# Branch projections by seven products of halves, with the weight sums of gates and branches kept in HBM

## The chip, the cores and the metric

The kernel runs on one core of a Trainium2 chip. The metric is the device time of one execution in microseconds (us). Three runs of the kernel before took 737.32, 737.47 and 738.17 us; the median is 737.47 us.

## The reference, cut to what matters

The program is one layer of a token mixer and a feed-forward block on an input of 512 tokens by 1024 channels, all in float32. Three mixers give `ya`, `yb` and `yc`, each 512 by 512. Each goes through a branch projection and is weighed by a gate:

```python
h = _rmsnorm(x, norm_mix[l])
p = h @ w_in[l]
u, v, bg, cg, xb, zc, gl = jnp.split(p, splits, axis=-1)
...
g = jax.nn.sigmoid(gl).reshape(bn, s, N_BRANCH, D_MODEL)
merged = (g[:, :, 0] * (ya @ w_br_a[l])
          + g[:, :, 1] * (yb @ w_br_b[l])
          + g[:, :, 2] * (yc @ w_br_c[l]))
x = x + merged @ w_o[l]
h = _rmsnorm(x, norm_ffn[l])
a = _causal_dwconv(h @ w_up[l], ffn_conv_w[l])
ag, av = jnp.split(a, 2, axis=-1)
x = x + (jax.nn.silu(ag) * av) @ w_down[l]
```

`w_br_*` are 512 by 1024, each gate's part of `w_in` is 1024 by 1024, `w_o` is 1024 by 1024, `w_up` is 1024 by 5632 and `w_down` 2816 by 1024.

## The kernel before, in words

**Arithmetic.** Every float32 operand of a matmul is split into a high part (a rounded copy by ScalarE, `upper`, line 59) and a low part (the rest, by VectorE, `lower`, line 67). One product of a 128x128 block with 128x512 columns is then three matmuls, high by high, high by low and low by high (`mm3`, lines 81 to 83).

**Stages**, in the order of the work: the head (x is turned, v is projected), ten column blocks of the input projections (u, z, cg, xb, bg; 1 MB of `w_in` each as two loads of 512 KB), three rounds of a gate and a branch projection, the output projection (`po`), eleven pairs of blocks of the up projection (`pug`, `puv`), the down projection (`da`, `dd`, `db`, `de`, `df`) and the final norm.

**Gates.** A gate's 512x1024 by 1024x1024 product is made of seven products of halves instead of eight (lines 877 to 925): tokens in two halves, k in two halves, output columns in two halves. The sums of activations are made on VectorE (`form`, lines 712 to 777). The sums of weights are made while loading: GpSimd issues DMAs that add a quarter of `w_in` to a buffer already in SBUF (`add_weights`, line 749; `gate_pieces`, lines 824 to 854). Each of the seven products is four k blocks of 128 by 512 columns, times two token blocks.

**Branches.** A branch projection is done plainly (lines 950 to 966): for each of two halves of 512 columns, four k blocks times four token blocks, `mm3` each. The projection comes after its gate; `weigh` (line 940) multiplies its PSUM bank with the gate on VectorE and adds it to the sum.

**Weights on their way.** `Raws` (lines 95 to 121) issues loads on SyncE's queue (line 109) in a fixed order, into buffers `raw` of 128x1024; a load is issued when the buffer it takes has been split. Four buffers are live in the input and up stages and eight in the gate stage (`raws.cap`, lines 781 and 967). `Pieces` (lines 247 to 267) splits a piece up to three ahead of its use into a ring; in the gate stage the ring is four slots of 128x512, in the up and down stages four slots of 128x1024.

**GpSimd.** Beside the adding DMAs it has some elementwise work in the input stage: `v - mu` (line 437), `row1_sq` (line 577), the four sums of the longest pooling window (line 633) and `cv * row1` (line 700). Its DMAs and what has to keep its place among them are chained by `in_order` (line 741).

**Down projection.** It uses seven products of halves too. Its four weight sums `t1` to `t4` are made in HBM by DMAs that GpSimd issues: a copy of a quarter of `w_down`, then a DMA that adds another quarter or sum to it (lines 1019 to 1022). They are 2816 KB each and run after the last gate's adding DMAs. SyncE later loads `t1` to `t4` as it loads weights.

Of the kernel before, what the change touches and what calls it, by code (L numbers as in the profile page):

```python
# [7 lines left out]
F32 = mybir.dt.float32  # L8
# [18 lines left out]
def trunk_kernel(  # L27
# [58 lines left out]
    RAWS = 8  # L86
# [3 lines left out]
    def extra_slots(name):  # L90

        return [[rawp.tile([P, 1024], F32R, tag="raw", name=f"{name}_{p}{i}") for p in ("hi", "lo")]
                for i in range(2)]
# [29 lines left out]
    raws = Raws()  # L123

# [51 lines left out]
    w_br = [w[0].rearrange("(k p) c -> p k c", p=P) for w in (w_br_a, w_br_b, w_br_c)]  # L176
# [9 lines left out]

    def rows(name, view, k, c0):
        raws.add(name, view[:, k:k + 2, c0:c0 + 512])
# [15 lines left out]
    for i in range(3):  # L204
        g0 = 3072 + 1024 * i

        for name, kh, h in (("w", 0, 0), ("x", 0, 0), ("v", 1, 0), ("y", 0, 1), ("z", 1, 1)):
            for kp in range(2):
                rows(f"g{i}{name}{kp}", w_in_v, 4 * kh + 2 * kp, g0 + 512 * h)
        for h in range(2):  # L210
            for kp in range(2):
                rows(f"br{i}{h}{kp}", w_br[i], 2 * kp, 512 * h)
    for h in range(2):
        for kq in range(4):
            rows(f"o{h}{kq}", w_o_v, 2 * kq, 512 * h)
    for name, view, c0 in col_blocks[n_in:]:
        cols(name, view, c0)

# [28 lines left out]
    class Pieces:  # L247
        def __init__(self, slots, ahead):
            self.slots, self.n_ahead = slots, ahead
            self.sources, self.done, self.taken = [], 0, 0  # L250
# [25 lines left out]
    first = extra_slots("first")  # L276
    slots = own + first
# [35 lines left out]
    load_v(6, 2)  # L313

# [118 lines left out]
    def v_center():  # L433
        nc.vector.tensor_scalar(mu, mu, 1.0 / 64, None, op0=ALU.mult)
        for t in range(NT):
            v3 = by_group(vs[t])
            nc.gpsimd.tensor_tensor(v3, v3, spread_group(mu, t), op=ALU.subtract)
# [101 lines left out]
    v_center()  # L539

# [25 lines left out]
    for b in range(2):  # L566
        w = blocks.take(f"u{b}")
        for j in range(2):
# [28 lines left out]
    ya = [pair(f"ya{c}", f"ya{c}") for c in range(4)]  # L597

    def spatial(q):
# [15 lines left out]
        nc.vector.tensor_tensor(t0, t0, uT[q], op=ALU.mult)  # L615
        split(ya[q][0], ya[q][1], t0)


    yc = [pair(f"yc{c}", f"yc{c}") for c in range(4)]
    PAD = 16  # L620

    def pooled(g, o):
# [6 lines left out]
        for step in range(g + 1):  # L629
# [3 lines left out]
            (nc.gpsimd if g == 3 else nc.vector).tensor_tensor(s2[:, lo:], s[:, lo:], s[:, lo - d:PAD + S - d], op=ALU.add)  # L633
# [11 lines left out]
    def pool_map(g, plr):  # L645
        o2 = bank(f"pyc{g}")
        mm3(o2, [p[:, g * P:(g + 1) * P] for p in pw], plr, True, True)
        nc.scalar.activation(yc[g][0], o2, AF.Copy, scale=p_scale(g))
        nc.vector.scalar_tensor_tensor(
            yc[g][1], o2, p_scale(g), yc[g][0].bitcast(F32), op0=ALU.mult, op1=ALU.subtract  # L650
        )
# [13 lines left out]
    yb = [pair(f"yb{c}", f"yb{c}") for c in range(4)]  # L665
    for b in range(2):
# [29 lines left out]
        for j in range(2):  # L696
# [13 lines left out]


# [17 lines left out]

    temps = iter(("x01", "x10", "x11", "x20", "x21", "x30", "x31", "x01"))  # L730
# [4 lines left out]
    def tt(o, a, b, op):  # L735
        return nc.vector.tensor_tensor(o, a, b, op=op)


    last_of_pool = []

    def in_order(ins):
        if last_of_pool:
            tc.add_manual_dep(
                ins.ins, last_of_pool.pop().ins.name,
                mybir.DependencyInfo(mybir.DependencyClass.NoSync, mybir.DependencyReason.DATA),
                reason="in the order written")
        last_of_pool.append(ins)

    def add_weights(t, view):
        in_order(nc.gpsimd.dma_start(t.rearrange("p (a b) -> p a b", b=view.shape[2]), view, accum_op=ALU.add))  # L750
# [28 lines left out]
    halves = [[t[:, 512 * c:512 * c + 512] for t in s] for s in own for c in range(2)]  # L779
    pieces = Pieces(halves, 3)  # L780
    raws.cap = RAWS

    def plain_piece(name, k, last, after=None):

        held = {}

        def source(slot):
            raw = raws.get(name) if k == 0 else source.raw()
            held["raw"] = raw
            split(*slot, raw[:, 512 * k:512 * k + 512])  # L790
            if last:
                raws.free()
            if after:
                after()

        source.held = held
        return source

    def block_pieces(name, after=None):
        a = plain_piece(name, 0, False)  # L800
        b = plain_piece(name, 1, True, after)
        b.raw = lambda: a.held["raw"]
        pieces.add(a)
        pieces.add(b)

# [489 lines left out]
```

## Time and profile before

| | |
|---|---|
| median of 3 runs | 737.47 us |
| the profiled execution, its own time | 737.11 us |
| its span on the core | 735.2 us |
| TensorE matmul (PE) busy | 725.7 us, 99% |
| VectorE (DVE) busy | 538.6 us, 73% |
| ScalarE (ACT) busy | 344.6 us, 47% |
| GpSimd (POOL) busy | 65.6 us, 9% |
| DMA queue q1 (issued by SyncE and ScalarE) | 88.90 MB, 38.1% of 16 engines |
| DMA queue q0 (issued by GpSimd) | 35.65 MB, 23.0% of 16 engines |

The page calls the engines PE, DVE, ACT, POOL and SP. Matmuls overlap, so that one of 128x512 is shown as lasting 389 ns while the next starts some 0.23 us later; time on TensorE is counted here by starts. A view of a stretch ("window") gives times from the start of the span. In the rows, a name like `pug` stands for all tiles of that name, `<-` separates what is written from what is read, and `L109` is a line of the kernel.

### The profile page before, as it was taken

The numbers are of one execution on the slowest core, as the hardware profiler recorded it, in microseconds if no ns is written. First come the engines' busy times: TensorE is split into PE (matmuls) and PEld (weight loads), VectorE is DVE, ScalarE is ACT, GpSimd is POOL, SyncE is SP. The second block draws the span as 40 slices with busy tenths as digits, with TensorE's granted clock in tenths as the row PEclk, the third lists the DMA queues.
The fourth block names the chain that finished last, engine by engine and source line by source line (L and its number), as shares of the span: only waits on it lengthen the run. The fifth ranks groups of instructions, "written<-read, shape, count | busy, mean of one in ns | idle before, by whom it ended". The sixth has DMA issues, their size and how long they took to land.

```text
span 735.2 us, 9006 instructions
## 1 busy us (share of the span) xinstructions
PE 725.7 (99%) x3294; PEld 600.9 (82%) x3294; DVE 538.6 (73%) x841; ACT 344.6 (47%) x537; POOL 65.6 (9%) x74
## 2 busy tenths in 40 slices
PE   8999999999999999999999999999999999999996
PEld 6888888888888888888888888888888888888885
DVE  6789799656556676765666886766787776998684
ACT  4744243246435525624544443443444444966453
POOL 0030202320121112101010000000000000001010
PEclk9999999999999999999999999999999999999999
DMA  7643122889879779999999963323233222576652
GB/s 256 183 138 92 52 87 84 202 198 232 228 157 214 198 169 193 365 249 360 234 241 313 221 180 101 100 86 115 87 92 108 87 101 86 153 240 194 193 164 115
DMA packets 79627, 126.24 MB, mean 172 GB/s; under 512 B 3639, under 2 KB 38879, under 8 KB 79583
## 3 DMA queue, kind: packets, MB, share of 16 engines
q1 hardware_dynamic: 64527, 88.90, 38.1%
q0 software_dynamic: 14336, 35.65, 23.0%
q10 hardware_dynamic: 720, 1.11, 0.4%
q8 instruction: 26, 0.43, 0.3%
q14 instruction: 18, 0.15, 0.1%
HBM read 120.41 MB, written 25.17 MB: 198 GB/s over the span
## 4 chain that ended last, share of the span: by engine, by line
PE 98%; DVE 1%; DMA 1%; ACT 0%; issue 0%; ACTq 0%
PE pug L83 5%; PE puv L83 5%; PE pug L81 5%; PE puv L81 5%; PE puv L82 5%; PE pug L82 5%; PE pbr L81 3%; PE pbr L82 3%; PE pbr L83 3%; PE po L81 2%; PE po L83 2%; PE po L82 2%; PE gb L82 1%; PE gb L81 1%; PE gd L82 1%; PE gd L81 1%
## 5 line engine op out<-in xcount | busy, mean ns | idle before, releaser
L81 PE MATMUL pug<-h2T_hi,second_hi 128*128 128x512 f32 x176 | 68.7, 390 | 0.0
L83 PE MATMUL pug<-h2T_hi,second_lo 128*128 128x512 f32 x176 | 68.5, 389 | 0.0
L82 PE MATMUL puv<-h2T_lo,ring_hi 128*128 128x512 f32 x176 | 68.5, 389 | 0.0
L81 PE MATMUL puv<-h2T_hi,ring_hi 128*128 128x512 f32 x176 | 68.5, 389 | 0.0
L82 PE MATMUL pug<-h2T_lo,second_hi 128*128 128x512 f32 x176 | 68.5, 389 | 0.0
L83 PE MATMUL puv<-h2T_hi,ring_lo 128*128 128x512 f32 x176 | 68.5, 389 | 0.0
L67 DVE TENSOR_TENSOR ring_lo<-raw_uv,ring_hi 128x1024 fp32r<-128x1024 f32 x22 | 26.9, 1221 | 25.1 <-ACT ring_hi L59 25.1
L59 ACT CAST second_hi<-raw_ug 128x1024 fp32r<-128x1024 f32 x22 | 23.2, 1055 | 43.1 <-PE pug L82 42.3
L82 PEld LDWEIGHTS puv<-h2T_lo,ring_hi 128*128 128x128 f32 x176 | 33.0, 188 | 6.9
L83 PEld LDWEIGHTS pug<-h2T_hi,second_lo 128*128 128x128 f32 x176 | 33.0, 188 | 6.9
L82 PEld LDWEIGHTS pug<-h2T_lo,second_hi 128*128 128x128 f32 x176 | 33.0, 188 | 6.9
L83 PEld LDWEIGHTS puv<-h2T_hi,ring_lo 128*128 128x128 f32 x176 | 33.0, 188 | 6.9
L81 PEld LDWEIGHTS puv<-h2T_hi,ring_hi 128*128 128x128 f32 x176 | 33.0, 188 | 6.9
L81 PEld LDWEIGHTS pug<-h2T_hi,second_hi 128*128 128x128 f32 x176 | 33.0, 188 | 6.8
L1142 POOL TENSOR_TENSOR xr<-xr,gain_f 128x512 f32<-128x512 f32 (+1 forms) x5 | 7.6, 1529 | 312.1 <-ACT sf L145 312.1
L67 DVE TENSOR_TENSOR ring_lo<-raw_br,ring_hi 128x512 fp32r<-128x512 f32 x24 | 16.6, 690 | 21.6 <-ACT ring_hi L59 21.6
L59 ACT CAST ring_hi<-raw_uv 128x1024 fp32r<-128x1024 f32 x22 | 23.2, 1054 | 19.2 <-PE puv L82 19.0
L67 DVE TENSOR_TENSOR second_lo<-raw_ug,second_hi 128x1024 fp32r<-128x1024 f32 x22 | 26.9, 1222 | 3.1 <-ACT second_hi L59 3.0
L1036 ACT ACTIVATE av<-av_y,colv 128x512 f32<-128x512 f32 x22 | 15.9, 724 | 27.9 <-DVE av_y L1034 26.9
L59 ACT CAST ring_hi<-raw_br 128x512 fp32r<-128x512 f32 x24 | 14.9, 620 | 26.0 <-PE pbr L83 18.8
L1036 ACT ACTIVATE ag<-ag_y,colv 128x512 f32<-128x512 f32 x22 | 15.7, 717 | 21.5 <-DVE ag_y L1034 21.5
L81 PE MATMUL po<-ring_hi,mg_hi 128*128 128x512 f32 x64 | 25.7, 401 | 0.0
(537 smaller groups left out, 2056.6 us busy)
## 6 DMA issues: line engine op xcount, KB each, us to landing
down_t<-in_w_down_dram POOLq DMA_DIRECT2D x6, 2816.0 KB, 27.9
raw_ug<-in_w_up_dram SPq DMA_DIRECT2D x22, 512.0 KB, 3.6
raw_uv<-in_w_up_dram SPq DMA_DIRECT2D x22, 512.0 KB, 3.5
raw_m<-down_t SPq DMA_DIRECT2D x20, 512.0 KB, 4.3
raw_m<-in_w_down_dram SPq DMA_DIRECT2D x15, 512.0 KB, 4.0
down_t<-down_t POOLq DMA_DIRECT2D x2, 2816.0 KB, 21.5
raw_o<-in_w_o_dram SPq DMA_DIRECT2D x8, 512.0 KB, 10.7
raw_u<-in_w_in_dram SPq DMA_DIRECT2D x4, 512.0 KB, 3.5
```

Of the source, the lines that this page charges most:

```text
L59: return keep(nc.scalar.copy(hi, src))
L67: return keep(nc.vector.tensor_tensor(lo, src, hi.bitcast(F32), op=ALU.subtract))
L81: keep(nc.tensor.matmul(o, st[0], mv[0], start=first, stop=False, **skip))
L82: keep(nc.tensor.matmul(o, st[0], mv[1], start=False, stop=False, **skip))
L83: keep(nc.tensor.matmul(o, st[1], mv[0], start=False, stop=last, **skip))
L1036: nc.scalar.activation(a, y, AF.Copy, scale=ffn_w(2, c))
L1142: nc.gpsimd.tensor_tensor(y, y, gain3[h][:, cut], op=ALU.mult)
```

## The change

It does these things:

- A branch projection is made of seven products of halves (`branch`), each of two k blocks times two token blocks, from sums of activations (`branch_forms`) and of weights. It now comes ahead of its gate, and its results `c` wait in SBUF; the gate multiplies them in. `ya`, `yb` and `yc` are no longer split, their forms are.
- In gate, branch and down projection the products M1, M6, M7 and M4 go into one PSUM bank pair `x` (M1 with its sign turned by its weights), which is copied out between (`copies`); M5 and M3 share another, M2 has a third.
- All weight sums of gates and branches are made in HBM (`WeightSums`): four tiles `t1` to `t4` for each, copied (`copy`) and added to (`add`) by DMAs of GpSimd. The copies for the first branch are issued once the last load of v's weights is there, the rest in a row after `v_center`. The adding DMAs into SBUF go away.
- Gate and branch weights are loaded and split as pieces of 128x1024, in a ring of four slots; the ring takes four more of the raw buffers for good, and four raw buffers are left.
- The down projection's sums are issued once x has been loaded again for the residual (`pool_waits_for`), copy and add by turns as before.
- The elementwise work of lines 577, 633 and 700 goes from GpSimd to VectorE.
- The output projection takes its k blocks in the order 4 to 7, 0 to 3, with some of the transposes (`turn`) within the gate and between its steps.

The diff, cut to its core:

```diff
-    RAWS = 8
+    own += [[rawp.tile([P, 1024], F32R, tag="raw", name=f"ring_{p}{i}") for p in ("hi", "lo")]
+            for i in range(2, 4)]
...
+    class WeightSums:
+        def __init__(self, name, b11, b12, b21, b22):
+            t1, t2, t3, t4 = self.t = [
+                dram.tile([P, b11.shape[1], 528], F32, name=f"{name}_t{i + 1}")[:, :, :512] for i in range(4)]
+            self.base = [(t1, b11), (t3, b12), (t2, b22), (t4, b21)]
+            self.added = [(t1, b12), (t3, b22), (t2, t1), (t4, t2)]
+
+            self.products = (("m1", b11), ("m5", t1), ("m6", t2), ("m2", b21), ("m7", t3), ("m3", b22), ("m4", t4))
+
+        def copy(self, n=4):
+            for t, w in self.base[:n]:
+                in_order(nc.gpsimd.dma_start(t, w))
+            del self.base[:n]
+
+        def add(self, n=4):
+            for t, w in self.added[:n]:
+                in_order(nc.gpsimd.dma_start(t, w, accum_op=ALU.add))
+            del self.added[:n]
...
     class Pieces:
...
         def take(self, n=1):
-
             i = self.taken
             self.taken += n
-            self.ahead(i + max(n, 1 + self.n_ahead))
-            got = [self.slots[k % len(self.slots)] for k in range(i, i + n)]
-            return got if n > 1 else got[0]
+            self.ahead(i + len(self.slots))
+            return [self.slots[k % len(self.slots)] for k in range(i, i + n)]
...
+    pool_waits_for(wv_raw[3], "begun")
+    branch_sums[0].copy()
...
     v_center()
+    for i in range(3):
+        branch_sums[i].copy()
+        branch_sums[i].add()
+        gate_sums[i].copy()
+        gate_sums[i].add()
...
-                nc.gpsimd.tensor_tensor(row1_sq, row1, row1, op=ALU.mult)
+                nc.vector.tensor_tensor(row1_sq, row1, row1, op=ALU.mult)
...
-            (nc.gpsimd if g == 3 else nc.vector).tensor_tensor(s2[:, lo:], s[:, lo:], s[:, lo - d:PAD + S - d], op=ALU.add)
+            nc.vector.tensor_tensor(s2[:, lo:], s[:, lo:], s[:, lo - d:PAD + S - d], op=ALU.add)
...
-            nc.gpsimd.tensor_tensor(cv[j], cv[j], row1, op=ALU.mult)
-            nc.vector.tensor_tensor(cv[j], o, cv[j], op=ALU.mult)
-            split(yb[c][0], yb[c][1], cv[j])
+            nc.vector.tensor_tensor(cv[j], cv[j], row1, op=ALU.mult)
+            nc.vector.tensor_tensor(yb[c], o, cv[j], op=ALU.mult)
...
+    pieces = Pieces(slots)
+    for i in range(3):
+        add_seven(f"br{i}", branch_sums[i], pieces)
+        add_seven(f"g{i}", gate_sums[i], pieces)
...
+    def branch_forms(i):
+        got = []
+        tags = list(free_tags)
+        for b in range(2):
...
+            even, odd = ys[i][2 * b:2 * b + 2]
+            s12, s34 = [scratch(3, f"s{n}_{i}{b}") for n in ("12", "34")]
+            tt(half(s34, 0), half(even, 1), half(even, 0), ALU.subtract)
+            tt(half(s12, 0), half(even, 1), half(odd, 1), ALU.subtract)
+            tt(half(s12, 1), half(odd, 1), half(s34, 0), ALU.subtract)
+            tt(half(s34, 1), half(odd, 0), half(s12, 1), ALU.subtract)
+            a11 = act.tile([P, 2, 256], F32R, tag=tags.pop(0), name=f"a11_{i}{b}")
+            split(a11[:, 0], a11[:, 1], half(even, 0))
+            f12, f34, fo = parts("f12"), parts("f34"), parts("fo")
+            split(*f12, s12)
+            split(*fo, odd)
+            split(*f34, s34)
...
+    def copies(tag, name, o):
+        got = [scratch(tag, f"{name}{r}") for r in range(2)]
         for r in range(2):
-            nc.scalar.copy(m1[r], a[r])
...
+            nc.scalar.copy(got[r], o[r])
+        return got
...
+    def gate(i, c):
...
+        x = banks(f"gx{i}")
+        product(x, of_quarter(0, 0), 4, True)
+        m1 = copies(0, f"m1{i}", x)
+        d = banks(f"gd{i}")
+        product(d, of_form(s1), 4, True)
+        m5 = copies(1, f"m5{i}", d)
+        product(x, of_form(s2), 4, False)
+        m16 = copies(2, f"m16{i}", x)
+        a = banks(f"ga{i}")
+        product(a, of_quarter(1, 0), 4, True)
         for r in range(2):
-            add(m15[r], d[r], m1[r], ALU.subtract)
...
+            tt(m1[r], a[r], m1[r], ALU.subtract)
+            sigmoid(r, m1[r], m1[r])
+            weigh(r, 0, m1[r])
+        product(x, of_form(s3), 4, False)
...
+    def branch(i, form):
...
+        x = banks(f"bx{i}")
+        product(x, form("a11"), 2, True)
+        m1 = copies(0, f"bm1{i}", x)
+        d = banks(f"bd{i}")
+        product(d, form("s1"), 2, True)
+        m5 = copies(1, f"bm5{i}", d)
+        product(x, form("s2"), 2, False)
+        m16 = copies(2, f"bm16{i}", x)
+        a = banks(f"ba{i}")
+        product(a, form("a12"), 2, True)
+        for r in range(2):
+            tt(c[r][0], a[r], m1[r], ALU.subtract)
+        product(x, form("s3"), 2, False)
+        for r in range(2):
+            tt(c[2 + r][1], x[r], m5[r], ALU.add)
+        product(d, form("s4"), 2, False)
+        for r in range(2):
+            tt(c[r][1], d[r], m16[r], ALU.add)
+        product(x, form("a22"), 2, False)
+        for r in range(2):
+            nc.scalar.mul(c[2 + r][0], x[r], -1.0)
+        return c
...
     for i in range(3):
-        sg = gate(i)
+        c = branch(i, forms[i])
...
+    down_sums = WeightSums("d", *quarters(lambda k: w_dn_q[k], 0))
+    for t in range(NT):
+        for c in range(2):
+            pool_waits_for(xr[t][c], f"begun{t}{c}")
+    for n in range(4):
+        down_sums.copy(1)
+        down_sums.add(1)
```

`pool_waits_for(t, name)` is a copy of one column of `t` by GpSimd. `add_seven` puts the seven products' pieces in order, two k blocks to a piece, so that a branch's product is one piece and a gate's two.

## Rows read from the trace of the kernel before

**Rows 1.** The page: busy time of TensorE, and its chain that ended last.

```profile
PE 725.7 (99%) x3294; PEld 600.9 (82%) x3294; DVE 538.6 (73%) x841; ACT 344.6 (47%) x537; POOL 65.6 (9%) x74
...
PE 98%; DVE 1%; DMA 1%; ACT 0%; issue 0%; ACTq 0%
```

**Rows 2.** Waits of TensorE, the whole span: us in total, times, longest.

```profile
PE warm_ps L328 <- DVE warm L319: 1.6, 1, 1.6
PE tp L360 <- DMA x<-in_x_dram: 1.1, 1, 1.1
PE tm L934 <- DVE sg L944: 0.3, 1, 0.3
```

**Rows 3.** Tiles of the first gate and branch on TensorE: first and last start.

```profile
L81 PE MATMUL ga<-ring_hi,hT_hi x48: 389/389/389, 152.4 to 287.7; 128*128 128x512 f32 x48
...
L81 PE MATMUL pbr<-ring_hi,ya_hi x32: 389/389/389, 190.4 to 211.5; 128*128 128x512 f32 x32
```

**Rows 4.** Groups by line and form: a slot's split, a bank's copy and sum.

```profile
L59 ACT CAST ring_hi<-raw_uv 128x1024 fp32r<-128x1024 f32 x22 | 23.2, 1054 | 19.2 <-PE puv L82 19.0
L67 DVE TENSOR_TENSOR ring_lo<-raw_uv,ring_hi 128x1024 fp32r<-128x1024 f32 x22 | 26.9, 1221 | 25.1 <-ACT ring_hi L59 25.1
...
L896 ACT COPY m<-ga 128x512 f32<-128x512 f32 x6 | 3.4, 589 | 0.6 <-PE ga L83 0.3
...
L890 DVE TENSOR_TENSOR m<-gd,m 128x512 f32<-128x512 f32 x6 | 3.8, 682 | 0.0
```

**Rows 5.** DMA in 322 to 330 us: an adding DMA, and loads of 2 KB rows.

```profile
q0 software_dynamic: 539, 1.10, 74.2%
q1 hardware_dynamic: 508, 0.94, 36.1%
```

**Rows 6.** DMA in 336 to 342 us: a copying DMA, and loads of 2 KB rows.

```profile
q1 hardware_dynamic: 425, 0.78, 34.3%
q0 software_dynamic: 414, 1.67, 68.8%
```

**Rows 7.** DMA in 413 to 424 us: an adding DMA, and loads of 1 KB rows.

```profile
q0 software_dynamic: 827, 1.69, 83.2%
q1 hardware_dynamic: 815, 0.82, 27.5%
```

**Rows 8.** DMA in 397 to 403 us: a copying DMA, and loads of 1 KB rows.

```profile
q0 software_dynamic: 492, 2.02, 81.6%
q1 hardware_dynamic: 488, 0.48, 22.9%
```

**Rows 9.** DMA in 305.5 to 313 us, between a copying and an adding DMA.

```profile
q1 hardware_dynamic: 1342, 2.58, 96.6%
q0 software_dynamic: 40, 0.09, 6.3%
```

**Rows 10.** GpSimd in order of time: start, length, what.

```profile
44.41 4.05 POOL L437 TENSOR_TENSOR v<-v,mu 128x512 f32<-128x512 f32 x4 [23.91 <-DVE mu L434]
...
288.12 1.44 POOL L1021 DMA_DIRECT2D down_t<-in_w_down_dram  x1
307.83 1.72 POOL L1022 DMA_DIRECT2D down_t<-in_w_down_dram  x1 [18.27 <-DMA down_t<-in_w_down_dram]
308.71 1.94 POOL L1021 DMA_DIRECT2D down_t<-in_w_down_dram  x1
```

**Rows 11.** Time to landing of loads: `raw_o` beside sums, `raw_z` without.

```profile
DMA to landing us min/median/max: 10.3/10.7/11.1
...
DMA to landing us min/median/max: 4.0/4.3/4.6
```

**Rows 12.** Busy us in windows: PE, PEld, DVE, ACT, POOL, clock, DMA share, GB/s.

```profile
48.00:152.00 104.00, 104.00 (x487) 87.14 (x486) 88.30 (x146) 38.15 (x56) 17.16 (x12) 1.00 0.37 104
152.00:330.00 178.00, 178.00 (x791) 147.40 (x790) 115.15 (x180) 85.79 (x138) 28.52 (x25) 1.00 0.90 224
...
383.00:624.00 241.00, 241.00 (x1067) 199.42 (x1066) 178.20 (x264) 102.83 (x147) 1.49 (x1) 1.00 0.46 130
```

**Rows 13.** Groups by line: work that moves off GpSimd, and splits that go.

```profile
L700 POOL TENSOR_TENSOR cva<-cva,n_row 128x512 f32<-128x512 f32 x4 | 6.7, 1681 | 33.9 <-DVE cva L692 33.9
...
L67 DVE TENSOR_TENSOR ya_lo<-sgt,ya_hi 128x512 fp32r<-128x512 f32 x4 | 2.7, 686 | 0.7 <-ACT ya_hi L59 0.7
```

More of the change, by code (lines that the diff above doesn't have):

```diff
@@ L123, in trunk_kernel, with in_order, add_seven, add_block @@
     raws = Raws()
+    last_of_pool = []
+    def in_order(ins):
+        if last_of_pool:
+            tc.add_manual_dep(
+                ins.ins, last_of_pool.pop().ins.name,
+                mybir.DependencyInfo(mybir.DependencyClass.NoSync, mybir.DependencyReason.DATA),
+                reason="in the order written")
+        last_of_pool.append(ins)
+    class WeightSums:
[13 more added lines that the diff above has]
+            del self.added[:n]
+    NEGATIVE = ("m1", "m4")
+    def add_seven(name, weights, pieces):
+        for m, w in weights.products:
+            n = w.shape[1]
+            for q in range(0, n, 2):
+                add_block(f"{name}_{m}_{q}", w[:, q:min(q + 2, n)], pieces,
+                          split_negative if m in NEGATIVE else split)
+    def add_block(name, view, pieces, cut):
+        raws.add(name, view)
+        def source(slot):
+            raw = raws.get(name)
+            n = view.shape[1] * view.shape[2]
+            cut(*[s[:, :n] for s in slot], raw[:, :n])
+            raws.free()
+        pieces.add(source)
     def rsqrt(v, shape, name):
@@ L594, in trunk_kernel @@
     split(pw[0], pw[1], pw_raw)
-    ya = [pair(f"ya{c}", f"ya{c}") for c in range(4)]
+    ya = [act.tile([P, S], F32, tag=f"ya{c}hi", name=f"ya{c}") for c in range(4)]
     def spatial(q):
@@ L614, in spatial @@
                 )
-        nc.vector.tensor_tensor(t0, t0, uT[q], op=ALU.mult)
-        split(ya[q][0], ya[q][1], t0)
-    yc = [pair(f"yc{c}", f"yc{c}") for c in range(4)]
+        nc.vector.tensor_tensor(ya[q], t0, uT[q], op=ALU.mult)
+    yc = [act.tile([P, S], F32, tag=f"yc{c}hi", name=f"yc{c}") for c in range(4)]
     PAD = 16
@@ L662, in trunk_kernel @@
                 spatial(g - 2)
-    yb = [pair(f"yb{c}", f"yb{c}") for c in range(4)]
+    yb = [act.tile([P, S], F32, tag=f"yb{c}hi", name=f"yb{c}") for c in range(4)]
     for b in range(2):
@@ L777, in trunk_kernel @@
         split(*s4[kp], f2)
[L779 to L804, printed above, removed]
-    gate_blocks = {}
-    def fetch(i, of):
-        for kp in range(2):
-            gate_blocks[i, of, kp] = raws.get(f"g{i}{of}{kp}")
-    def add_quarter(i, of, kh, h):
-        g0 = 3072 + 1024 * i + 512 * h
-        for kp in range(2):
-            k = 4 * kh + 2 * kp
-            add_weights(gate_blocks[i, of, kp], w_in_v[:, k:k + 2, g0:g0 + 512])
@@ L928, in trunk_kernel, with product @@
-    mg = [[[act.tile([P, 4, P], F32R, tag=f"y{'ab'[c]}{t}{p}", name=f"mg{t}{c}_{p}") for p in ("hi", "lo")]
-           for c in range(2)] for t in range(NT)]
+    nrstd1 = small.tile([P, NT], F32, tag="nrstd", name="nrstd1")
+    nc.vector.tensor_scalar(nrstd1, rstd1, -1.0, None, op0=ALU.mult)
+    def product(o, st, n, first, last=True):
+        for q in range(0, n, 2):
+            [w] = pieces.take()
+            for k in range(q, q + 2):
+                mv = [p[:, 512 * (k - q):512 * (k - q) + 512] for p in w]
+                for r in range(2):
+                    mm3(o[r], st(k, r), mv, first and k == 0, k == n - 1, more=not first)
```

348 lines of the change are left out of this document (129 added, 219 removed).

## Prediction

> **What bounds the kernel now.** I read the page first, its busy times and its chain that ended last: TensorE is busy 725.7 of 735.2 us, and the chain is 98% TensorE [rows 1]. Then the waits of TensorE: over the whole span they are a few us in the head and one of 0.3 us where the branches end [rows 2]. So every matmul taken away is worth its time, and every wait put before one costs its own. The pace comes from the tiles: 31 steps of three matmuls from the first to the last start of the first branch, 190.4 to 211.5 us, give 21.1 / 93 = 0.227 us for a matmul of 128x512 [rows 3]. Last the DMA views. The gate stage already has its DMA engines at 0.90 of their time, the input stage at 0.37 and the up stage at 0.46 [rows 12]. That is where this change puts new work.
>
> **What the change takes away.** A branch has 2 x 4 x 4 x 3 = 96 matmuls; by seven products of two k blocks and two token blocks it has 7 x 2 x 2 x 3 = 84. Three branches lose 36, at 0.227 us: **-8.2 us**, all of it on the path. Gates, down and output projections keep their matmuls and transposes.
>
> **Work that moves beside TensorE.** GpSimd's nine elementwise operations of lines 577, 633 and 700 go to VectorE, at about 0.69 us each there (GpSimd took 1.68 for line 700 [rows 13]): +6.2 us. The splits of `ya`, `yb` and `yc` go, twelve like `ya_lo` at 0.69: -8.3 us [rows 13]. The forms of the first branch come: eight sums of half width, two splits of half width and six full ones, some 8.5 us by halves and wholes of the same 0.68. VectorE then has about 88.3 + 6.4 = 95 us to do in the 104 of the input stage [rows 12]; ScalarE has room. The cover is thin but there; if it failed, each us over would be one on the path. In the gate stage, lower halves cost as much in whole slots (21 x 1.221 a round against 36 x 0.69), the small sums stay alike, and two sets of forms come: VectorE goes from 115 in 178 us [rows 12] to some 135 in 170. I cost both stages at nothing. The down projection loses a few sums on VectorE, which nothing waits for.
>
> **The sums in HBM.** Each gate's four sums are four copies and four additions of 1.05 MB, each branch's half of that; the copies for the first branch go early, and the rest is queued at GpSimd from 48.5 us on, when `v - mu` is done [rows 10]. The trace has such DMAs, those for `w_down`, and shows what they do to loads on the other queue. With both queues at work, they get as many packets as each other: 539 and 508, 414 and 425, 827 and 815, 492 and 488 [rows 5 to 8]. What differs is what a packet carries. Beside loads of 1 KB rows an addition moves 1.69 MB / 11 us = 154 GB/s and a copy 337; beside loads of 2 KB rows it is 137 and 278. The loads get 75 to 80 GB/s in rows of 1 KB and 118 to 130 in rows of 2 KB [rows 5 to 8]. Between a copy and the addition that waits for it, the sums leave a hole of some 7 us in which loads run at 2.58 / 7.5 = 344 GB/s [rows 9]. In the change `t4` waits for `t2`, so a set has one such hole, and the next set's copies stand behind `t4` on GpSimd's queue.
>
> With these rates: the first branch's additions last 14 us and a hole of 7, to 69 us; the first gate 12 + 27 + 7, to 116; the second branch 20 + 7, to 143; then beside 2 KB loads the second gate 15 + 31 + 7, to 195; the third branch 23 + 7, to 225; the third gate 46, to 271. The first branch begins at 152.4 us, where the first gate does now [rows 3].
>
> *Input stage, to 152 us.* A block of 48 matmuls lasts 10.9 us and takes two loads, 96 GB/s, against the 75 to 80 left. The up stage has the same demand beside the same kind of sums, and TensorE is busy there for 241.0 of 241 us [rows 12]: four live loads and the holes cover it. Cost nothing; with no holes the shortage of 18 GB/s over 75 us would be 1.35 MB, under three loads.
>
> *Branches and gates.* A piece of 128x1024 serves 12 matmuls, 2.72 us, so TensorE uses 0.524 / 2.72 = 193 GB/s. From 152 to 271 us sums run for 105 us and leave two holes, 14 us. Beside them loads get some 125 GB/s: short by 68 x 105 = 7.1 MB, 13.6 pieces. The holes give back (344 - 193) x 14 = 2.1 MB, 4.0 pieces. The stock is four loaded buffers and three split slots ahead; with one on its way, six. What is left, 13.6 - 4.0 - 6 = 3.6 pieces, is waited for: **+9.8 us**. Ends: at the better 134 GB/s and with seven in stock it is 11.8 - 4.0 - 7 = 0.8 pieces, 2 us, and sums that end 10 us sooner make it nothing; with a stock of three and no use of the holes it is 10.6 pieces, 29 us. I take the middle sum, for its terms come from the same kind of DMA. The longer landing is in the trace too: 10.7 us for `raw_o` beside sums, 4.3 for `raw_z` without [rows 11]; with four live buffers of 0.524 MB, 10.7 us just feed 196 GB/s.
>
> The adding DMAs into SBUF that go away took queue time from loads that had eight buffers; no wait on TensorE goes with them [rows 2]. SyncE's queue is in order: a load of a sum not yet made holds every load behind it. The third gate begins at 152.4 + 2 x 57.2 + 19.1 = 286 us, and its first sum is loaded some 19 us before use, at 272, when `t1` has been ready for 30 us; `t4` is asked for at about 300. No wait, with a margin of some 30 us.
>
> *The down sums* start when the residual's x is back, some 50 us later than the 288 of now [rows 10], and last until about 480; they are loaded from 620 on. They lie in the up stage wholly, at the cover named above.
>
> **Hand-offs in the branch.** The pair `x` is filled, copied and filled again one product later, and that product lasts only 12 x 0.227 = 2.72 us. ScalarE needs two copies of 0.589 and has at most one split of 1.054 ahead: 2.23 us. VectorE needs two sums of 0.682 and one `lower` of 1.221: 2.59 us [rows 4]. Both fit, the second barely. The nearest rows show no such wait; the ends are nothing, and one more split ahead at all nine hand-offs, 9 x 1.22 = 11 us. I take **+2 us**, near the low end, since the queues are some 80% full and not more.
>
> **Sum.** Against the profiled execution's own 737.1 us: -8.2 + 9.8 + 2.0 = 740.7 us. The median of the runs is 0.4 higher, so **741.0 us** as the others are measured. 0.2%, 1.5 us, is about what a measurement of this kernel can tell from no change.
>
> **The rivals.**
>
> *The loads keep pace: faster.* The place is the stretch from 152 to 271 us; the point from which it decides is some 145 GB/s for loads while sums run (105 x 48 = 5.0 MB, 9.6 pieces, all held by stock and holes). Then only the 36 matmuls count, with 0 to 2 us of hand-offs: 729 to 731 us. For it: copies and loads together move 408 to 417 GB/s [rows 6, 8], and the sum above misses only 3.6 of 63 pieces. Against it: packets go one for one [rows 5 to 8], and an addition and loads together move 228 to 255 GB/s only [rows 5, 7]. 30%. The Trainium skill, page "DMA: Bandwidth & Descriptors", section "Where 436 GB/s comes from", has the 16 ports carry 435 GB/s; the 77 MB of sums and loads of 48 to 324 us would be 280 GB/s, well inside, and the time this rival's. By that rule copies agree with it and additions don't, at 255.
>
> *It cancels:* the wait is 4 to 8 us: 736 to 739 us. 10%.
>
> *Hand-offs and forms:* the narrow products stall TensorE, in place of the loads or beside them, 5 to 11 us: 734 to 740 without the loads' waits. Against it: the sums of rows 4. 6%.
>
> *Sums too late:* no row shows an addition of rows 24 KB apart; if these ran at 100 GB/s instead of 137 to 154, 18.9 MB would take some 55 us longer, 25 us past the margin, and the SyncE queue would stand still behind them: 755 to 775 us. 8%.
>
> *The forecast:* contention costs more than the matmuls bring, 738.5 to 755 us. 46%. That the matmuls don't go can be left out: their count is in the loops.
>
> **How the numbers follow.** The likeliest case gives 741.0, its own range 738.5 to 755. Faster by over 0.2% is the first rival and a third of the hand-off case: 0.32. Within 0.2%: the middle of the cancelling case and a little of the forecast's edge, 0.11. Slower: the forecast, the late sums and the rest: 0.57. The range for 8 in 10 takes in the fast case from 730 and the forecast's tail to 757; half of the late sums and a part of the fast case's lower edge lie outside.
>
> **What would show it.** In the profile after: 84 matmuls a branch; packets of both queues near one for one until about 270 us, DMA share near 1.0; waits of TensorE in the first two gates and the second branch, on splits whose loads landed late, and none in the third gate; none in input and up stage. Wrong would be a third gate that waits for its sums, waits on `copies` in the branches with loads long landed, or no wait at all, with the span 8 us shorter.

## The result, and the profile after

The change made the kernel slower: 755.95 us (median of 4 runs, 754.62 to 760.18) against 737.39, a ratio of 1.026 [1.0218, 1.0301]. The sign was forecast, and 755.95 lies inside the range for 8 in 10 (730 to 757). But the forecast was +3.6 us, and the kernel lost 18.6, just beyond the forecast case's own 738.5 to 755. The profiled execution took 760.18 us, the slowest of the four, with a span of 758.4; 4.2 us of what it shows are its own.

The page of the kernel after, busy times, queues, HBM and chain:

```profile
PE 728.3 (96%) x3258; PEld 595.7 (79%) x3258; DVE 554.5 (73%) x828; ACT 367.9 (49%) x540; POOL 69.3 (9%) x98
...
q1 hardware_dynamic: 70239, 99.91, 41.0%
q0 software_dynamic: 23168, 60.82, 33.3%
...
HBM read 159.73 MB, written 62.91 MB: 294 GB/s over the span
...
PE 76%; DMA 16%; DVE 4%; ACT 1%; issue 1%; SPq 0%; ACTq 0%; DVEq 0%
```

The 36 matmuls are gone (3294 to 3258), yet the span is longer. The chain was 98% TensorE before [rows 1]; now DMA holds 16% of it.

Where it went is read from first starts on TensorE. The tiles `pu` (first block of the input stage), `bx` (first branch), `po` (output projection) and `pug` (up projection) of the kernel after:

```profile
L81 PE MATMUL pu<-hT_hi,ring_hi x32: 389/389/504, 39.0 to 60.8; 128*128 128x512 f32 x32
...
L81 PE MATMUL bx<-ring_hi,a x12: 389/389/389, 158.0 to 297.5; 128*128 128x512 f32 x12
...
L81 PE MATMUL po<-ring_hi,mg_hi x64: 389/389/497, 357.0 to 404.9; 128*128 128x512 f32 x64
...
L81 PE MATMUL pug<-h2T_hi,ring_hi x176: 389/389/478, 405.9 to 634.9; 128*128 128x512 f32 x176
```

Before, `pu` started at 33.4 us, the first gate at 152.4 [rows 3], `po` at 336.0 and `pug` at 383.0. So the input stage (from `pu` to the first branch or gate) is unchanged, 119.0 us both times. The head grew by 5.6 us in this execution, and the three rounds grew from 183.6 to 199.0 us although they hold fewer matmuls.

The windows of the kernel after, columns as in [rows 12]:

```profile
20.00:40.00 20.00, 17.00 (x73) 13.27 (x72) 11.70 (x21) 11.55 (x25) 0.30 (x1) 0.91 0.64 228
48.00:152.00 104.00, 104.00 (x486) 87.06 (x486) 94.69 (x166) 38.55 (x55) 25.23 (x28) 1.00 0.94 242
152.00:180.00 28.00, 26.73 (x119) 21.83 (x118) 16.17 (x21) 13.90 (x20) 3.43 (x3) 1.00 1.07 295
...
200.00:220.00 20.00, 15.90 (x64) 11.21 (x63) 10.86 (x12) 11.25 (x13) 3.02 (x3) 1.00 1.07 324
220.00:240.00 20.00, 15.56 (x68) 12.62 (x67) 12.89 (x18) 13.35 (x20) 6.29 (x7) 0.95 1.02 355
240.00:260.00 20.00, 19.09 (x73) 14.88 (x72) 12.94 (x19) 7.81 (x11) 1.04 (x1) 0.88 1.09 269
...
383.00:624.00 241.00, 241.00 (x1074) 199.34 (x1073) 172.74 (x255) 101.69 (x149) 12.74 (x15) 1.00 0.72 194
```

TensorE has no idle time in the input stage and the up stage, as forecast, though the DMA engines are at 0.94 and 0.72 there. It loses 4 us in each of the two windows from 200 to 240. (A matmul counts as busy for 389 ns at a pace of 227, so each wait is partly hidden in these columns.)

Its waits over the whole span (total, times, longest):

```profile
PE bx L81 <- ACT bm L886: 6.8, 2, 4.4
PE pv L81 <- ACT hT_hi L59: 3.0, 1, 3.0
PE gx L81 <- DVE m L790: 3.0, 2, 1.9
PE gd L82 <- DVE ring_lo L67: 2.6, 5, 0.8
PE bx L81 <- DVE c L790: 2.0, 2, 1.3
PE gx L82 <- DVE ring_lo L67: 1.9, 4, 0.8
...
PE gx L81 <- ACT m L886: 0.9, 1, 0.9
```

Of the 17.2 us in the rounds (all but `pv`), 12.7 name not a split (`ring_lo`) but a copy or a sum of a bank (`bm`, `m`, `c`). For 9.3 of them a late load stands behind it all the same. The longest, in the second branch, as TensorE's and ScalarE's timelines show it:

```profile
239.57 0.79 PE L81 MATMUL bx<-ring_hi,f_hi 128*128 128x512 f32 x1 [4.44 <-ACT bm L886]
```
```profile
232.84 1.05 ACT L59 CAST ring_hi<-raw_br_m 128x1024 fp32r<-128x1024 f32 x1 [3.01 <-DMA raw_br_m<-br_t]
...
237.47 1.04 ACT L59 CAST ring_hi<-raw_br_m 128x1024 fp32r<-128x1024 f32 x1 [1.79 <-DMA raw_br_m<-in_w_br_b_dram]
...
238.94 1.06 ACT L886 COPY bm<-bx 128x512 f32<-128x512 f32 x2
```

In its timeline ScalarE takes one operation after the other, in the kernel's order. The piece that this product needs came 3.01 us late and was split at 232.84 us. But the product also needs bank `bx` copied out, and that copy stands behind the split of the next piece, whose load came 1.79 us late. So one late load stops both the product that needs it and a product that doesn't.

The other 3.4 us (1.05 and 2.32) came after the sums. The last addition landed at 281.1 us (12.4 us after its issue), and no split waited for its load from 283 to 306 us. VectorE then worked almost without a gap, 23.66 of 24 us, and a copy of `bx` waited for it (window, columns as above; ScalarE; TensorE):

```profile
282.00:306.00 24.00, 19.80 (x83) 15.53 (x84) 23.66 (x32) 16.10 (x23) 0.00 (x0) 1.00 0.56 174
```
```profile
302.73 1.19 ACT L886 COPY bm<-bx 128x512 f32<-128x512 f32 x2 [1.76 <-DVE c L790]
```
```profile
303.37 0.50 PE L81 MATMUL bx<-ring_hi,f_hi 128*128 128x512 f32 x1 [2.32 <-ACT bm L886]
```

The queues in 157 to 178 us, a gate's additions (and, up to some 162 us, the end of its copies) beside loads of 2 KB rows (packets, MB, busy share):

```profile
q0 software_dynamic: 1398, 3.32, 72.4%
q1 hardware_dynamic: 1271, 2.45, 34.9%
```

That is nearly packet for packet again, as in [rows 5], and leaves the loads 2.45 / 21 = 117 GB/s where TensorE uses 193. GpSimd's timeline shows how long it lasts, here the last additions of the second gate and the third gate:

```profile
188.24 1.01 POOL L150 DMA_DIRECT2D g_t<-g_t  x1 [14.90 <-issue]
...
268.67 1.01 POOL L150 DMA_DIRECT2D g_t<-g_t  x1 [15.07 <-issue]
```

### The profile page after: what moved, and what is told of

Its sections match the earlier page's. It is cut to its first block, busy times and chain, and to the rows that moved or that the text cites. A ratio compares the mean times of both kernels' runs of the same rounds, so it can differ in the third digit from the quotient of the medians.

```text
span 758.4 us, 8935 instructions
## 1 busy us (share of the span) xinstructions
PE 728.3 (96%) x3258; PEld 595.7 (79%) x3258; DVE 554.5 (73%) x828; ACT 367.9 (49%) x540; POOL 69.3 (9%) x98
## 4 chain that ended last, share of the span: by engine, by line
PE 76%; DMA 16%; DVE 4%; ACT 1%; issue 1%; SPq 0%; ACTq 0%; DVEq 0%
DMA raw_g_m<-in_w_in_dram 6%; PE pug L81 5%; PE puv L81 5%; PE pug L83 5%; PE puv L83 5%; PE puv L82 5%; PE pug L82 5%; DMA raw_g_m<-g_t 4%; DMA raw_br_m<-in_w_br_b_dram 3%; PE dx L83 2%; PE dx L81 2%; PE po L81 2%; PE dx L82 2%; PE po L83 2%; PE po L82 2%; DVE ring_lo L67 2%
## 5 line engine op out<-in xcount | busy, mean ns | idle before, releaser
L81 PE MATMUL pug<-h2T_hi,ring_hi 128*128 128x512 f32 x176 | 68.7, 390 | 0.0
L83 PE MATMUL pug<-h2T_hi,ring_lo 128*128 128x512 f32 x176 | 68.5, 389 | 0.0
L82 PE MATMUL pug<-h2T_lo,ring_hi 128*128 128x512 f32 x176 | 68.5, 389 | 0.0
L67 DVE TENSOR_TENSOR ring_lo<-raw_g_m,ring_hi 128x1024 fp32r<-128x1024 f32 x30 | 36.5, 1224 | 42.4 <-ACT ring_hi L59 42.3
L59 ACT CAST ring_hi<-raw_g_m 128x1024 fp32r<-128x1024 f32 x30 | 31.3, 1052 | 43.0 <-DMA raw_g_m<-g_t 20.9
L67 DVE TENSOR_TENSOR ring_lo<-raw_d_m,ring_hi 128x1024 fp32r<-128x1024 f32 (+1 forms) x30 | 35.4, 1194 | 9.0 <-ACT ring_hi L59 8.9
L59 ACT CAST ring_hi<-raw_d_m 128x1024 fp32r<-128x1024 f32 (+1 forms) x30 | 29.4, 980 | 19.1 <-PE da L83 8.2
L83 PEld LDWEIGHTS pug<-h2T_hi,ring_lo 128*128 128x128 f32 x176 | 33.0, 188 | 7.0
L82 PEld LDWEIGHTS pug<-h2T_lo,ring_hi 128*128 128x128 f32 x176 | 33.0, 188 | 6.8
L81 PEld LDWEIGHTS pug<-h2T_hi,ring_hi 128*128 128x128 f32 x176 | 33.0, 188 | 6.8
L59 ACT CAST ring_hi<-raw_uv 128x1024 fp32r<-128x1024 f32 x22 | 23.2, 1054 | 19.2 <-PE puv L82 19.0
```

The costliest lines, as they stand in the source:

```text
L59: return keep(nc.scalar.copy(hi, src))
L67: return keep(nc.vector.tensor_tensor(lo, src, hi.bitcast(F32), op=ALU.subtract))
L81: keep(nc.tensor.matmul(o, st[0], mv[0], start=first, stop=False, **skip))
L82: keep(nc.tensor.matmul(o, st[0], mv[1], start=False, stop=False, **skip))
L83: keep(nc.tensor.matmul(o, st[1], mv[0], start=False, stop=last, **skip))
```

## The experiments

One number is compared throughout, from each profiled execution: the time from the first branch's first start to that of `po`, less the 173.2 us it takes in the run without sums (first experiment), less 2.7 us for each branch of plain tiles. It is called the rounds' loss. For the kernel after it is 357.0 - 158.0 - 173.2 = 25.8 us. It is that of one execution, and the profiled ones lie 1.9 us below to 4.2 us above their kernel's median (the kernel after: 4.2 above). So a difference of a few us in it ranks no two kernels; the medians do.

**No sums.** The products load plain quarters in place of sums. This kernel leaves the sums out and so computes something else; only its time counts.

```
+            if plain:
+                self.base, self.added = [], []
+                t1, t2, t3, t4 = b12, b22, b12, b21
```

> Part left out: the weight sums of gates and branches; the pieces that would read a sum read a plain quarter of the same size instead, so loads, splits and matmuls stay alike and no copying or adding DMA runs before the down projection's. Theory (sums take the loads' turns on the DMA engines, and the early copies hold up the head): the head is back at 33.4 us, the three rounds lose nearly all of their 25 us of waits (4 us or less left), the time is 729 to 735 us. Rival (the short products' hand-offs between TensorE, ScalarE and VectorE): over 10 us of waits stay in the rounds, 740 us or more.

Measured: 730.4 us, ratio 0.9904 [0.9889, 0.9918]. First starts:

```profile
L81 PE MATMUL bx<-ring_hi,a x12: 389/390/390, 153.4 to 269.7; 128*128 128x512 f32 x12
```
```profile
L81 PE MATMUL po<-ring_hi,mg_hi x64: 388/390/497, 326.6 to 374.5; 128*128 128x512 f32 x64
```

TensorE has no wait after the head. So the sums are the whole loss: 25.5 us between the two medians, the head's part included. The new products, forms and hand-offs cost nothing while loads are on time. This is what was expected.

**The early copies later.** The first branch's copies are issued with the other sums.

```
-    pool_waits_for(wv_raw[3], "begun")
-    branch_sums[0].copy()
```

> One part undone: the four copies for the first branch are no longer issued in the head but with the others after v - mu. Theory for the head: the load of the pooling weights lands as early as in the kernel before, pu begins at 33.4 us instead of 39.0, and the first set of sums takes some 6 us longer, which is paid back in part by more overlap later: 749 to 754 us. Rival (the head's delay has another cause, and the early copies cost nothing): pu still begins at 39 us and the time is 756 us or more.

Measured: 756.93 us, ratio 1.0268 [1.0249, 1.0287]: a miss, since the time is the rival's, though the head is the theory's. ScalarE waits for the load of `pw_raw`, with the early copies beside it (kernel after), and without them (this run):

```profile
28.44 0.62 ACT L59 CAST pw_hi<-pw_raw 128x512 fp32r<-128x512 f32 x1 [8.59 <-DMA pw_raw<-in_pool_w_dram]
```
```profile
21.32 0.62 ACT L59 CAST pw_hi<-pw_raw 128x512 fp32r<-128x512 f32 x1 [1.62 <-DMA pw_raw<-in_pool_w_dram]
```

The head is back (`pu` at 34.0 us), but the rounds' loss is 356.0 - 152.9 - 173.2 = 29.9: the last addition is issued at 269.22 us (268.67 in the kernel after), while the first branch starts 5.1 us sooner, so more of the sums lies beside the rounds. What is won in the head is lost there, as far as one execution of each shows. Nor do the early copies cost the head 5.6 us each time: in the five kernels of this study that keep them, `pu` starts at 34.4 to 39.0 us, in the others at 33.4 to 35.4.

**A second load queue.** Every second load of the rounds is issued by ScalarE.

```
-                nc.sync.dma_start(t[:, :n].rearrange("p (a b) -> p a b", b=view.shape[2]), view)
+                self.count = getattr(self, "count", 0) + 1
+                queue = nc.scalar if name[0] in "bg" and "_m" in name and self.count % 2 else nc.sync
+                queue.dma_start(t[:, :n].rearrange("p (a b) -> p a b", b=view.shape[2]), view)
```

> Every second load of gate and branch weights is issued by ScalarE instead of SyncE, so that loads come on two queues beside the sums' one; nothing else is changed. Theory (each queue with work gets as many packets as any other): while sums run, loads get up to two packets in three, some 170 GB/s instead of 125, the waits in the rounds fall from 25 to under 12 us, the sums end 20 us later or more, and the time is 741 to 749 us. Rival (the engines are full by bytes, whoever asks): loads and sums keep their shares, 753 us or more, with ScalarE's queue held up besides.

Measured: 744.09 us, ratio 1.0091 [1.0076, 1.0106], 11.9 us less than the change, rounds' loss 12.7. The same window, 157 to 178 us:

```profile
q0 software_dynamic: 1281, 2.82, 66.0%
q10 hardware_dynamic: 816, 1.57, 21.2%
q1 hardware_dynamic: 726, 1.41, 20.3%
```

Loads move 2.98 MB in place of 2.45, sums 2.82 in place of 3.32; the last addition is issued at 279.85 us in place of 268.67, 11 us later and not 20. The sums have that time, the loads had not. In 165 to 175 us, beside additions alone, the loads move 167 GB/s in place of 127, near the expected 170.

**Sums early.** All sums are queued from some 30 us on; `v - mu` moves to VectorE, the early copies go.

```
+    pool_waits_for(ss1[:, 7:8], "begun")
+    for i in range(3):
+        branch_sums[i].copy()
...
     rstd1 = all_rstd(ss1, "n1")
...
     v_center()
-    for i in range(3):
-        branch_sums[i].copy()
...
```

> The sums are queued as soon as the last load of the head has come, at some 30 us, with v - mu on VectorE in place of GpSimd; the early copies in the head go. Theory (what counts is how much of the sums' time falls on the branches and gates): all sums end 12 to 18 us sooner, the waits in the rounds fall by 5 to 12 us and the head is back at 33.4 us: 738 to 746 us. Rival (the waits come from the rounds themselves): only the head's 5 us are won, 749 us or more.

Measured: 746.26 us, ratio 1.0129 [1.011, 1.0148], just over the theory's 738 to 746; rounds' loss 341.9 - 153.3 - 173.2 = 15.4. The last addition is issued 18 us sooner, at 250.64 us, so less of the same traffic lies beside the rounds.

**Close rows.** A partition's rows of a sum lie behind one another in HBM.

```
-                dram.tile([P, b11.shape[1], 528], F32, name=f"{name}_t{i + 1}")[:, :, :512] for i in range(4)]
...
+                dram.tile([P, b11.shape[1] * 512 + 16], F32, name=f"{name}_t{i + 1}")[:, :b11.shape[1] * 512]
+                .rearrange("p (k c) -> p k c", c=512) for i in range(4)]
```

> The sums t of gates and branches lie close (a partition's rows of 2 KB one behind the other), so that a load of a sum has rows of 4 KB where it had 2 KB; the loads of plain weights keep 2 KB. Theory (the queues get one packet each, so the bytes of a queue follow its packet size): four of seven loads get near twice the bytes beside sums; TensorE's waits between the first branch and the output projection fall from some 25 us to under 8 and the time to 738 to 746 us, the head's 5 us still in it. Rival (sums and loads together are held to 228 to 261 GB/s whatever the packets): what the loads gain the sums lose, the sums end after 300 us in place of some 281, and the time stays at 748 to 757 us.

Measured: 749.32 us, ratio 1.0177 [1.0136, 1.0218]; rounds' loss 19.2, not under 8. Both theories missed: the time is the rival's, but the sums ended sooner, not later (last addition at 260.12 us). The edit also gave long rows to the sums' own additions, `t2 + t1` and `t4 + t2`.

**Early and two queues.** Both edits above.

> Both remedies at once: the sums queued from some 30 us on with no early head copies (744 to 748 us by itself), and every second load of the rounds on ScalarE's queue (743 to 745 us by itself). Theory (a shortage of loads beyond the stock, so that each remedy takes a part of the same sum away and the rest falls under what the stock holds): waits in the rounds under 6 us, 731 to 737 us. Rival (both buy the same time, since a faster load slows the sums and these end later): 740 to 745 us.

Measured: 739.88 us, ratio 1.0027 [1.0013, 1.0042]; rounds' loss 338.8 - 152.9 - 173.2 = 12.7, not under 6, in an execution 2.1 us above the median. The two remedies add up only in part, and the time is nearer the rival's 740 to 745 than the theory's 731 to 737.

**Early, two queues and close rows.** All three edits above.

> Early sums, two load queues and the close rows together. Theory (loads short beside sums is the only loss): no wait in the rounds beyond 2 us, 730 to 734 us, as with no sums at all. Rival (loads that take more make the sums so late that SyncE stands behind a load of an unfinished sum): waits in the third gate, over 738 us.

Measured: 748.92 us, ratio 1.0156 [1.0132, 1.018]: worse by 9 us than without close rows. The third gate waited for no sum. The queues in 152 to 185 us without close rows, and with them:

```profile
q0 software_dynamic: 1813, 3.65, 61.4%
q1 hardware_dynamic: 1352, 2.61, 23.2%
q10 hardware_dynamic: 1290, 2.51, 21.3%
```
```profile
q0 software_dynamic: 1239, 4.43, 62.4%
q1 hardware_dynamic: 947, 2.32, 20.2%
q10 hardware_dynamic: 807, 2.31, 18.7%
```

A packet of the sums grew from 2.0 to 3.6 KB, one of the loads from 1.9 to 2.6. So the sums took 0.78 MB more, and the loads got 0.49 MB less: here the longer rows went to the wrong side. From 152 to 281 us the loads moved 21.21 MB in place of 22.29, two pieces less, some 5.6 us of the 9 at TensorE's pace; the rest isn't accounted for. With close rows alone, on one load queue, it was the other way round: 20.81 MB of loads in 152 to 281 us, 18.94 in the kernel after, with sums that ended sooner. Why the same edit helps there and harms here is not shown.

**Only the branches' sums.** The gates' products load plain quarters; this kernel, too, computes something else.

```
-  WeightSums(f"g{i}", *quarters(...))
+  WeightSums(f"g{i}", *quarters(...), plain=True)
```

> The branches' sums are made as in the change, the early copies in the head too; the gates' are not: their products load plain quarters in place of sums. A third of the sums' bytes is left, and it is over before or near the first branch. Theory (waits come only where the shortage exceeds the stock; the head's copies cost some 5 us by themselves): no waits in the rounds beyond 1 us, 734 to 737 us, the first input product some 5 us later than with no sums. Rival (each byte of sums costs its part, a third of the 25 us beside the head): 740 to 746 us.

Measured: 731.57 us, ratio 0.9921 [0.9906, 0.9936]; `pu` 1.7 us later than with no sums, not 5; rounds' loss 328.3 - 155.2 - 173.2 = -0.1. The last addition is issued at 120.47 us, before the first branch. A third of the bytes, where it ends before the rounds, costs next to nothing: the loss is not a price per byte.

**One branch by plain tiles,** with early sums and two queues: first the second branch (`ORDINARY = (1,)`), then the first (`(0,)`).

```
+        if i not in ORDINARY:
+            branch_sums[i].copy()
+            branch_sums[i].add()
...
+        if i in ORDINARY:
+            for h in range(2):
+                o = [bank(f"bo{i}{h}{t}") for t in range(NT)]
+                for kk in range(2):
+                    [w] = pieces.take()
+                    for k in range(2):
...
+                        for t in range(NT):
...
+                            mm3(o[t], st, mv, kk == 0 and k == 0, kk == 1 and k == 1)
```

> Early sums and two load queues (739.9 us), and the second branch by plain tiles again: 12 matmuls more (+2.7 us), half as many loads in that branch (one piece for 24 matmuls), and its 6.3 MB of sums gone, which took GpSimd's queue from some 97.8 to 126.7 us, so that all later sums come some 29 us sooner. Theory (loads are short beside sums once the stock is used up, and only there): the sums end near 250 us, the waits of some 12 us in the rounds fall under 4, and the time is 731 to 736 us, faster than the kernel before. Rival (the waits belong to the product form, its narrow products and hand-offs, and the two gates left keep theirs): 8 us of waits or more stay, 738 to 743 us.

Measured: 732.71 us, ratio **0.9929 [0.9912, 0.9945]** against the kernel before, so 0.7% faster than that kernel, and as expected. Rounds' loss 331.1 - 154.3 - 2.7 - 173.2 = 0.9. Busy times, TensorE's only wait after the head, its window of the rounds, and the last addition:

```profile
PE 722.4 (99%) x3270; PEld 597.9 (82%) x3270; DVE 545.4 (74%) x811; ACT 365.0 (50%) x533; POOL 59.0 (8%) x86
```
```profile
PE gx L81 <- DVE m L799: 0.7, 1, 0.7
```
```profile
152.00:330.00 178.00, 177.32 (x791) 146.72 (x790) 121.53 (x146) 108.19 (x143) 11.36 (x12) 1.00 0.85 254
```
```profile
231.28 1.02 POOL L152 DMA_DIRECT2D g_t<-g_t  x1 [16.54 <-issue]
```

> The same with the first branch by plain tiles in place of the second: the sums lose the stretch from some 30 to 55 us, so that all of them come 25 us sooner; the loads' relief inside the branch falls at 152 to 175 us, where the stock is still full. Theory: waits in the rounds of 2 to 7 us, 733 to 739 us; less good than the second branch, since relief comes where it is least needed. Rival (only the moment at which the sums end counts): as good as with the second branch, within 1 us.

Measured: 737.89 us, ratio 1.0002 [0.9988, 1.0016]. Its sums end even sooner (last addition at 225.74 us), yet the rounds lose 336.8 - 156.8 - 2.7 - 173.2 = 4.1 us, as the theory had it. So, as far as one execution of each shows, not only the end of the sums counts but where the loads are relieved. And here the cover of the input stage failed: 122.8 us from `pu` to the first branch in place of 119.0, with one long wait (and a granted clock of 0.97 over 50 to 100 us). That is more than half of the 5.2 us between the two medians. The wait:

```profile
PE pz L83 <- DVE ring_lo L67: 1.9, 1, 1.9
```

**All branches by plain tiles.** The change without its branch part, one queue, no early copies.

> The change without its branch part: all three branches by plain tiles (36 matmuls back, +8.2 us), half as many loads in them, no branch sums and no copies in the head; the gates' sums stay in HBM, all loads on one queue. Theory: the gates' sums fill 49 to some 180 us only, so the shortage lies almost wholly in the input stage and the first round: waits in the rounds under 3 us, 737 to 742 us, as long as the kernel before. Rival (the gates' sums alone, two thirds of the bytes, cost two thirds of the 25 us): 750 us or more.

Measured: 737.53 us, ratio 0.9994 [0.9985, 1.0003]: as long as the kernel before, rounds' loss 333.7 - 152.4 - 8.2 - 173.2 = -0.1. The last gate addition is issued at 180.56 us:

```profile
152.00:330.00 178.00, 178.00 (x795) 147.65 (x794) 101.02 (x115) 99.66 (x129) 2.06 (x2) 1.00 0.66 188
```

So the gates' sums in HBM cost nothing by themselves, nor do the branches', when they end that early. Only both together last long enough beside the rounds, and against products that load more.

**The second branch by plain tiles, nothing else.**

> The change with the second branch by plain tiles and nothing else: one load queue, sums queued as in the change, early copies kept. Sums then end some 30 us sooner (near 250 us), and the branch's loads halve for some 22 us, which is 4 pieces. Theory (loads short beside sums): 30 us at some 70 GB/s short are 4 pieces, with the branch's own 4 some 20 of the 25 us of waits: 3 to 8 us of waits are left, 735 to 743 us with the head's part and the 12 matmuls. Rival (the gain came from the early start and the second queue, and the plain branch only adds to them): over 746 us.

Measured: 739.81 us, ratio 1.0038 [1.0023, 1.0052], rounds' loss 335.0 - 155.2 - 2.7 - 173.2 = 3.9, both as expected; the last addition is issued at 242.19 us. This one edit takes back 16 of the 18.6 us.

## Why the prediction was right in sign and wrong in size

- **36 matmuls, -8.2: right.** With nothing lost in the rounds, these take 333.7 - 152.4 = 181.3 us with plain branches and 173.2 with the new products: 8.1 less. (From 183.6 before it is 10.4; 1.9 of the 2.2 us beyond the matmuls are turns that moved behind the start of `po`: `po` to `pug` grew from 47.0 to 48.9.)
- **Loads short beside sums, +9.8: the right mechanism, the wrong size; this is the step that failed.** The rounds' loss measured 25.8 us in the profiled execution; between the medians it is 25.5 together with the head. Up to 282 us, when the last addition had landed, it can be counted in pieces (window and load queue):

```profile
158.00:282.00 124.00, 110.71 (x457) 86.04 (x455) 71.62 (x91) 65.05 (x89) 16.36 (x19) 0.97 1.05 292
```
```profile
q1 hardware_dynamic: 9629, 18.56, 42.7%
```

At full pace TensorE uses 124 / 2.72 = 45.6 pieces in that time; 18.56 MB are 35.4. So loads were 10.2 pieces short, where the forecast had 13.6 - 4.0 = 9.6: the rate was right (150 GB/s with the holes, where the forecast's 125 and 344 give 151). But TensorE used 38 pieces (the window's 457 matmuls, twelve to a piece), where stock and loads together are 41.4. The forecast's stock, "three split slots ahead; with one on its way, six", was there when the first branch began (four pieces split, two more loaded or nearly so), but 2.6 of the six were used up: 7 us and not 16. Pieces on their way when the sums end are stock not used, and a load takes 12 us beside sums (median to landing of the gates' loads in the rounds). That gives 7.6 pieces, 20.7 us. The other 5.1 us came after the sums, 83 matmuls in 24 us where 106 have room, mostly while VectorE caught up; for that the forecast had no term. This split is counted from one trace, no run varied the stock or VectorE's work alone, and 2.5 us of it are the clock's (below); that the loss belongs to the sums is shown. (The forecast also left out the third gate's own hole of 7 us: by its own terms the sums end at 278 and not 271. They ended at 281.1.)
- **Hand-offs, +2: nothing by themselves,** as the run without sums shows. But the mechanism is there in another form. The forecast put one split of 1.054 us ahead of a copy and not the time for which ScalarE stands before a late load; copies and sums of banks make 12.7 of the 17.2 us of waits in the rounds, 9.3 behind late splits. The other 3.4 are close to its own sign of being wrong, "waits on `copies` in the branches with loads long landed": VectorE was behind, and that late loads put it there is argued, not varied. In the six other kernels that make all the sums, the third branch waits for a copy of `bx` in the same place, 0.5 to 2.3 us; without sums it doesn't.
- **Input stage at nothing: right here, with thin cover.** VectorE worked 94.69 us of the 104, where the forecast had 95 (its forms add up to 7.5 us by its own terms, not 8.5). It held in all kernels but the one with the plain first branch, where it lost 3.8 us.
- **Early copies and head at nothing: wrong by up to 5.6 us** in the profiled execution, some 2.4 on average between the kernels that keep the early copies and those that don't. The forecast looked at GpSimd's queue for them and not at the load of `pw_raw` beside them.
- **Sums too late: right,** no kernel had TensorE wait in the third gate. That 755.95 lies in this rival's 755 to 775 is chance.
- **Rivals.** "The loads keep pace" fell with the 17.2 us of waits in the rounds, and "it cancels" with them; "hand-offs and forms" fell with the run without sums. Of the rule that the first of them names (the Trainium skill, page "DMA: Bandwidth & Descriptors", section "Where 436 GB/s comes from": 435 GB/s): the rounds' windows of 20 and 28 us move 269 to 355 GB/s with the DMA engines at 1.02 to 1.09 of their time, so the engines were full far below that rate (405 GB/s in 230 to 240 us, where copies run).

## What to carry to other kernels

Work put on an idle DMA queue takes its share from the loads by packets, so price it as a stretch of time in which loads run at a known lower rate, and count a stock of buffers only in part against a shortage that lasts many times the stock (here 2.6 of six pieces). Two moves that are each free can cost 25 us together: look for the one stretch that both fill, and undo the smallest part there (here one branch of three, for 12 matmuls). A late load costs more than its own product where copies that free a bank stand behind its split on an engine that works in order.

## What the runs showed of the hardware that was not expected

- **A second queue changes the shares.** The Trainium skill, page "DMA: Bandwidth & Descriptors", section "Rules for kernel authors", says that spreading DMAs over issuing engines doesn't help bandwidth. The total agrees: 5.80 MB on three queues against 5.77 on two in 157 to 178 us. The share doesn't: loads on two queues beside the adding queue moved 142 GB/s in place of 117, and the kernel took 11.9 us less. The same page of the Trainium skill, section "Queues, rings and completion order", has each DMA engine go round its queues a whole packet at a time, and the counts 1398 and 1271, nearly one for one, agree; with three queues each load queue had fewer packets than the sums (816 and 726 to 1281), so they weren't always full.
- **The waits cost clock too.** TensorE stood idle for the 4.44 us before 239.57 us, and the granted clock fell (windows of 230 to 240 and 240 to 250 us, clock 0.90 and 0.76):

```profile
230.00:240.00 10.00, 5.56 (x24) 4.35 (x23) 3.63 (x6) 5.38 (x9) 2.37 (x2) 0.90 1.03 405
240.00:250.00 10.00, 9.26 (x31) 7.07 (x31) 5.64 (x8) 2.53 (x4) 0.00 (x0) 0.76 1.08 276
```

If the rest of full speed is time at the lower of its two levels, 1.2 GHz, that is 10 x (0.10 + 0.24) / 0.5 = 6.8 us. A part of it falls into the idle time and costs nothing. What it cost is the product that came next: its twelve matmuls, started at 239.57 us and followed by the next product at 244.82, took 5.25 us in place of 2.72, so 2.5 us. A group of it, 628 ns for a matmul that takes 389 elsewhere:

```profile
L82 PE MATMUL bx<-ring_lo,f_hi 128*128 128x512 f32 x4 | 2.5, 628 | 0.0
```

The head of the profiled execution has the same (0.91 in 20 to 40 us). The forecast had no such term.
- **Bigger packets are no gift to loads alone.** With early sums and two load queues, longer rows for what all queues move made the sums' packets grow more than the loads', and the kernel slower by 9 us (739.88 to 748.92); with one load queue the same rows made it 6.6 us faster (755.95 to 749.32).
